# Splitting weights into high and low parts two k-tiles at a time in a two-layer recurrent decoder trunk

## The chip, the cores and the metric

The kernel runs on one core of a Trainium2 chip. The core has a matrix engine (TensorE, PE in the profile, with its weight loads as PEld), a vector engine (VectorE, DVE), a scalar engine (ScalarE, ACT), GpSimd (POOL), SyncE (SP, which only issues transfers here), and 16 DMA engines that move data between device memory (HBM) and the on-chip memories SBUF and PSUM. Each engine runs its own instructions in the order in which they stand and meets the others through semaphores. The metric is the device time of one execution in microseconds, as the median of several runs; lower is better.

## The reference

The reference computes a trunk of two residual layers on 256 positions of width 2048, all in float32. Each layer has two mixers that share one input and one output projection (layer 0: RWKV-7 and gated DeltaNet; layer 1: Mamba-2 and RG-LRU), then a gated feed-forward block with a short causal convolution (width 5632), then a gate that adds a normalised per-layer embedding.

```python
for i in range(DEPTH):                       # DEPTH = 2, x is (1, 256, 2048)
    y = even_mixer(x, ...) if i % 2 == 0 else odd_mixer(x, ...)
    h = layer_norm(DN_ALPHA * x + y, ln1_g[i], ln1_b[i])
    h = layer_norm(DN_ALPHA * h + conv_ffn(h, ffn_up[i], ffn_conv_w[i], ffn_conv_b[i], ffn_down[i]), ln2_g[i], ln2_b[i])
    e = rms_norm(p[i] @ ple_proj[i], ple_norm_g[i])
    x = h + jax.nn.sigmoid(h @ ple_gate_w[i] + ple_gate_b[i]) * e
```

All weights together are about 500 MB and each is used once.

## The kernel before

**The weight stream.** Every large product multiplies float32 weights by float32 activations with matmuls on the type `float32r`, which keeps fewer bits. To keep the precision, each operand is split into a high part (a cast to `float32r`) and a low part (the value less its high part), and three products are added: high by high, high by low, low by high. The activations are split once. The weights are split as they stream in: `wlist` lists all loads in order, 968 of them. One load (a granule, `granule`) brings two k-tiles, each 128 rows by 512 columns (416 or 464 in two of the projections), into a tile `wr` of 512 KB; four `wr` buffers exist (`PF`). ACT casts a k-tile into a tile `wh` (`self.scalar.copy`), DVE subtracts it from the raw weights into `wl`. Before the change each of these handles one k-tile.

**How far ahead.** `weights(name, p, k)` is called just before the matmuls of k-tile j are written out; it calls `ahead(j)`, which writes the casts up to k-tile j+5 and the subtractions up to k-tile j+4. Six `wh` and five `wl` buffers exist, so the cast of j+5 needs the buffer of j-1 back from PE.

**The products.** `down` makes a product with the activations as the stationary operand, six matmuls of 512 columns for each k-tile (bank `pd`). `up2` makes one with the weights stationary: four matmuls of 512 columns on `wh`, then four of 256 on `wl` (bank `pu`). `whole` adds the two halves of a bank of `up2`, over a small buffer `ph`.

**The order of the rest.** Everything else (post-processing of a bank, the mixers' own recurrences with their small matmuls, the layer norms) is written as tasks. A list scheduler (`pick`, `fill`, `need`) runs when the program is built: with a table of estimated costs it puts the tasks' instructions between the weight stream's, so that a small matmul stands where its inputs should be ready. The result is one fixed order for each engine. The casts and subtractions of `ahead` are not tasks: they stand where `ahead` is called.

**The layer norms.** At the end of the output projection and of the feed-forward block (four places) the last panel's sums (`x<-x,pd`) and their statistics (`st`, `mv`) go through DVE, the inverse root (`rstd`) and a product (`nmr`) through POOL, then rows are normalised on DVE (`x<-x,mv,rstd`) and ACT (`x<-x,nmr,rstd`), transposed on PE (bank `xt`) and scaled and split into `h` by ACT and DVE (`lv`). The next projection's matmuls wait for `h`. `down` with `early` writes the last four k-tiles of the panel for one half of the positions first, and two small panels (`pp`) give PE something to do meanwhile.

The functions that the diff touches:

Of the kernel before, what the change touches and what calls it, by code (L numbers as in the profile page):

```python
# [8 lines left out]
F32 = mybir.dt.float32  # L9
F32R = mybir.dt.float32r  # L10
AF = mybir.ActivationFunctionType
ALU = mybir.AluOpType
# [15 lines left out]
WSHAPES = {  # L28
# [5 lines left out]
    "lora": (1, 8, 464), "inA": (12, 4, 512), "inB": (16, 4, 512), "out0": (4, 8, 512),  # L34
    "zdt": (5, 8, 416), "xbc": (12, 4, 512), "inD": (16, 4, 512), "out1": (4, 16, 512),
}
# [32 lines left out]
class Pack:  # L69


    def __init__(self):
        self.at, self.cols, self.n = {}, [], 0
# [392 lines left out]
class Trunk(Scheduler):  # L466
    def __init__(self, ctx, tc, h, at, out, wlist):
        super().__init__(tc.nc)
        self.nc, self.h, self.at, self.out = self, h, at, out
        nc = self  # L470
        self.wlist = wlist
        self.wq = {key: i for i, key in enumerate(wlist)}
        self.n_dma = self.n_hi = self.n_lo = 0
        self.wt, self.wraw, self.names = {}, {}, {}
        self.loads = deque()
        pool = lambda name, bufs, **kw: ctx.enter_context(tc.tile_pool(name=name, bufs=bufs, **kw))
        self.cst = pool("cst", 1)
        self.wpool = pool("wp", 1)
        self.big = pool("big", self.NBIG)
        self.tmp = pool("tmp", 1)  # L480
        self.pm = pool("pm", 4, space=PSUM)
        self.pqp = pool("pq", self.NPQ, space=PSUM)
        self.dram = pool("dr", 1, space=DRAM)
        self.x1 = self.dram.tile([S, D], F32, name="x1")
        self.panel = 0
        self.done, self.used = {}, {}
        self.ident = self.cst.tile([128, 128], F32, name="ident")
        self.pk = self.cst.tile([128, h["pk"].shape[1]], F32, name="pk")
        self.cc = self.cst.tile([128, h["cst"].shape[1]], F32, name="cc")
        self.mhalf = self.cst.tile([128, 1], F32, name="mhalf")  # L490
        nc.gpsimd.memset(self.mhalf, -0.5)
        self.ones = self.cst.tile([128, 128], F32, name="ones")
        nc.gpsimd.memset(self.ones, 1.0)
# [52 lines left out]
        self.used[name] -= 1  # L546


    PF, SP, NBIG, LATE = 4, 4, 73, 4

    def granule(self, between=None):
        name, p, g = self.wlist[self.n_dma]
# [14 lines left out]
    def follow(self, t, tag, n):  # L567
# [4 lines left out]
            self.written[t.tensor.name] = [((t.tensor.name, 0, 128, 0, 1 << 20), end, None)]  # L572
        names.append(t.tensor.name)

    def ahead(self, j):

        n = 2 * len(self.wlist)
        while self.n_hi < min(n, j + self.SP + 2):
            i = self.n_hi // 2
            while self.n_dma < min(len(self.wlist), i + self.PF):  # L580
                self.granule()
            r = self.wraw[i][:, self.n_hi % 2, :WSHAPES[self.wlist[i][0]][2]]
            hi = self.wpool.tile([128, 512], F32R, tag="wh", bufs=self.SP + 2, name="wh")[:, :r.shape[1]]
            self.follow(hi, "wh", self.SP + 2)
            self.scalar.copy(hi, r)
            self.wt[self.n_hi] = [hi, r]
            self.n_hi += 1
        while self.n_lo < min(n, j + self.SP + 1):
            hi, r = self.wt[self.n_lo]
            lo = self.wpool.tile([128, 512], F32R, tag="wl", bufs=self.SP + 1, name="wl")[:, :r.shape[1]]  # L590
            self.follow(lo, "wl", self.SP + 1)
            self.vector.tensor_tensor(lo, r, hi.bitcast(F32), op=ALU.subtract)
            self.wt[self.n_lo][1] = lo
            self.n_lo += 1

    def weights(self, name, p, k):
        j = 2 * self.wq[name, p, k // 2] + k % 2
        self.ahead(j)
        self.wraw.pop(j // 2 - 1, None)
        return self.wt.pop(j)  # L600

    def post(self, gen, prio=0.0):
# [81 lines left out]
    def whole(self, ps):  # L684

        if ps.shape[1] == 512:
            t = self.tmp.tile([128, 256], F32, tag="ph", bufs=4, name="ph")
            self.scalar.copy(t, ps[:, 256:512])
            self.vector.tensor_tensor(ps[:, 0:256], ps[:, 0:256], t, op=ALU.add)
        return ps[:, 0:256]  # L690
# [1286 lines left out]
```

## Time and profile before

| | before |
|---|---|
| median of 3 runs | 2926.04 us (2923.46 to 2926.42) |
| the profiled execution's own time | 2927.23 us |
| its span (first to last instruction) | 2925.5 us |
| PE busy | 2898.3 us, 99% |
| DVE busy | 2158.3 us, 74% |
| ACT busy | 1735.9 us, 59% |
| DVE subtractions `wl<-wr,wh` | 1936, together 1318.5 us |
| ACT casts `wh<-wr` | 1936, together 1180.1 us |
| PE waits for the end of another engine or transfer | 11 pairs, longest in total 6.9 us |

A busy share is the union of an engine's instructions over the span. A matmul's record is longer than the distance to the next one, since they overlap, so the pace of PE is read from the starts.

### The profile page before, as it was taken

The page shows a single profiled execution, that of the slowest core. Times are in us where ns is not written, and L with a number is a line of the kernel's source. Part 1 is how long each engine was busy: PE and PEld are TensorE (multiplying, and loading weights), DVE is VectorE, ACT ScalarE, POOL GpSimd, SP SyncE. Part 2 cuts the span into 40 slices and gives each one's busy share as a digit, 9 for nine tenths or more (in the row PEclk, how much of TensorE's full clock was granted, in tenths as well). Part 3 has the DMA queues.
Part 4 walks back from the last instruction along what each step waited for, and adds up shares of the span by engine and source line. Part 5 has one row for each costly group of instructions (what it writes and reads, how often), then busy time and mean ns, then how long its engine had stood idle before and what let it go on. Part 6 is the DMA issues. An engine that isn't in the chain of part 4 may idle for free.

```text
span 2925.5 us, 48428 instructions
## 1 busy us (share of the span) xinstructions
PE 2898.3 (99%) x16986; PEld 2484.3 (85%) x16986; DVE 2158.3 (74%) x4246; ACT 1735.9 (59%) x3320; POOL 192.2 (7%) x317
## 2 busy tenths in 40 slices
PE   9999999999999999999999999999999999999999
PEld 8887887888888888888898888888888888888887
DVE  7789898687777775557856899855787777765567
ACT  6644555466666665446556778844666666654464
POOL 0133212000000000000000011000000000000000
PEclk9999999999999999999999999999999999999999
DMA  8554456465555556655776555666655555565556
GB/s 275 187 147 124 145 174 199 136 208 187 185 190 187 188 187 223 194 192 183 222 230 194 190 183 160 213 193 193 205 187 190 187 188 187 187 223 190 197 183 194
DMA packets 164949, 556.31 MB, mean 190 GB/s; under 512 B 19416, under 2 KB 32520, under 8 KB 164704
## 3 DMA queue, kind: packets, MB, share of 16 engines
q1 hardware_dynamic: 152128, 514.67, 53.9%
q0 software_dynamic: 12576, 38.55, 4.8%
q8 instruction: 133, 2.18, 0.3%
q14 instruction: 112, 0.92, 0.1%
HBM read 542.80 MB, written 10.34 MB: 189 GB/s over the span
## 4 chain that ended last, share of the span: by engine, by line
PE 93%; issue 2%; DMA 2%; DVE 2%; POOL 1%; ACT 0%; SPq 0%; POOLq 0%; DVEq 0%; ACTq 0%
PE pu L363 53%; PE pd L363 35%; DMA T<-inv 1%; PE s L363 1%; PE iv L363 1%; PE Y L363 1%; PE at L363 1%; PE lg L363 0%; PE tT L363 0%; PE xt L363 0%; POOL rstd L363 0%; DMA inv<-ix 0%; DMA inv<-AB 0%; PE R L363 0%; DVE wl L363 0%
## 5 line engine op out<-in xcount | busy, mean ns | idle before, releaser
L363 DVE TENSOR_TENSOR wl<-wr,wh 128x512 fp32r<-128x512 f32 (+2 forms) x1936 | 1318.5, 683 | 631.4 <-PE pd L363 312.5
L363 ACT CAST wh<-wr 128x512 fp32r<-128x512 f32 (+2 forms) x1936 | 1180.1, 618 | 892.9 <-PE pd L363 455.3
L363 PE MATMUL pu<-h,wh 128*128 128x512 f32 (+1 forms) x2944 | 781.5, 385 | 0.2
L363 PEld LDWEIGHTS pu<-h,wh 128*128 128x128 f32 x2944 | 499.2, 189 | 62.3 <-DVE h L363 0.6
L363 PEld LDWEIGHTS pu<-h,wl 128*128 128x128 f32 x2816 | 437.0, 189 | 57.3
L363 PE MATMUL pu<-h,wl 128*128 128x256 f32 x2816 | 463.8, 281 | 0.0
L363 PE MATMUL pu<-x,wh 128*128 128x512 f32 (+2 forms) x1024 | 281.8, 388 | 6.7 <-ACT wh L363 5.2
L363 PE MATMUL pd<-wh,acth 128*128 128x512 f32 x704 | 273.9, 389 | 0.0
L363 PE MATMUL pd<-wl,acth 128*128 128x512 f32 x704 | 273.9, 389 | 0.0
L363 PE MATMUL pd<-wh,actl 128*128 128x512 f32 x704 | 273.9, 389 | 0.0
L363 PE MATMUL pu<-xT,wh 128*128 128x512 f32 x896 | 250.3, 398 | 1.0 <-ACT xb L363 0.6
L363 PE MATMUL pd<-wh,yT 128*128 128x512 f32 x768 | 241.2, 391 | 0.0
L363 PEld LDWEIGHTS pu<-x,wh 128*128 128x128 f32 (+1 forms) x1024 | 172.7, 189 | 29.1 <-ACT wh L363 5.2
L363 PE MATMUL pu<-x,wl 128*128 128x256 f32 (+1 forms) x960 | 172.4, 288 | 0.0
L363 PEld LDWEIGHTS pu<-xT,wh 128*128 128x128 f32 x896 | 153.2, 189 | 22.0 <-ACT xb L363 0.9
L363 PEld LDWEIGHTS pd<-wh,yT 128*128 128x128 f32 x768 | 144.2, 188 | 30.5 <-issue 1.0
L363 PEld LDWEIGHTS pu<-x,wl 128*128 128x128 f32 (+1 forms) x960 | 150.5, 189 | 20.6 <-issue 1.5
L363 PE MATMUL pd<-wh,h 128*128 128x512 f32 x512 | 162.4, 393 | 0.0
L363 PEld LDWEIGHTS pd<-wh,acth 128*128 128x128 f32 x704 | 132.1, 188 | 27.6
L363 PEld LDWEIGHTS pd<-wl,acth 128*128 128x128 f32 x704 | 132.1, 188 | 27.4
L363 PEld LDWEIGHTS pd<-wh,actl 128*128 128x128 f32 x704 | 132.1, 188 | 27.3
L363 PEld LDWEIGHTS pu<-xT,wl 128*128 128x128 f32 x896 | 137.7, 189 | 19.5 <-issue 0.7
(409 smaller groups left out, 3214.3 us busy)
## 6 DMA issues: line engine op xcount, KB each, us to landing
wr<-in_up SPq DMA_DIRECT2D x336, 512.0 KB, 3.3
wr<-in_dn SPq DMA_DIRECT2D x176, 512.0 KB, 3.6
wr<-in_out SPq DMA_DIRECT2D x96, 512.0 KB, 4.2
wr<-in_inB SPq DMA_DIRECT2D x64, 512.0 KB, 3.5
wr<-in_gw SPq DMA_DIRECT2D x64, 512.0 KB, 3.9
wr<-in_inD SPq DMA_DIRECT2D x64, 512.0 KB, 4.2
wr<-in_inA SPq DMA_DIRECT2D x48, 512.0 KB, 4.1
wr<-in_xbc SPq DMA_DIRECT2D x48, 512.0 KB, 4.0
```

Of the source, the lines that this page charges most:

```text
L363: getattr(x.eng, op.name)(*op.a, **op.k)
```

## The change

One cast and one subtraction now handle a whole granule, that is both k-tiles (128 x 2 x 512). `wh` and `wl` become tiles of two k-tiles with three buffers each (`HI`). At the even k-tile of granule g, `ahead` writes the cast of granule g+2; at the odd one the subtraction of granule g+2. Only the very first granule is still split in two steps (`apart`). In SBUF, `wh` takes the same room, `wl` 2 KB more for each partition, and the buffers of `ph` go from 4 to 2 to pay for it.

```diff
-    PF, SP, NBIG, LATE = 4, 4, 73, 4
+    PF, HI, NBIG, LATE = 4, 3, 73, 4
...
+    @staticmethod
+    def apart(i):
+
+        return [slice(0, 2)] if i else [slice(0, 1), slice(1, 2)]
+
     def ahead(self, j):
 
-        n = 2 * len(self.wlist)
-        while self.n_hi < min(n, j + self.SP + 2):
-            i = self.n_hi // 2
-            while self.n_dma < min(len(self.wlist), i + self.PF):
+        n, g = len(self.wlist), j // 2
+        while self.n_hi < min(n, g + self.HI):
+            i = self.n_hi
+            while self.n_dma < min(n, i + self.PF):
                 self.granule()
-            r = self.wraw[i][:, self.n_hi % 2, :WSHAPES[self.wlist[i][0]][2]]
-            hi = self.wpool.tile([128, 512], F32R, tag="wh", bufs=self.SP + 2, name="wh")[:, :r.shape[1]]
-            self.follow(hi, "wh", self.SP + 2)
-            self.scalar.copy(hi, r)
-            self.wt[self.n_hi] = [hi, r]
+            w = WSHAPES[self.wlist[i][0]][2]
+            hi = self.wpool.tile([128, 2, 512], F32R, tag="wh", bufs=self.HI, name="wh")
+            self.follow(hi, "wh", self.HI)
+            for a in self.apart(i):
+                self.scalar.copy(hi[:, a, :w], self.wraw[i][:, a, :w])
+            self.whi[i] = hi
             self.n_hi += 1
-        while self.n_lo < min(n, j + self.SP + 1):
-            hi, r = self.wt[self.n_lo]
-            lo = self.wpool.tile([128, 512], F32R, tag="wl", bufs=self.SP + 1, name="wl")[:, :r.shape[1]]
-            self.follow(lo, "wl", self.SP + 1)
-            self.vector.tensor_tensor(lo, r, hi.bitcast(F32), op=ALU.subtract)
-            self.wt[self.n_lo][1] = lo
+        while self.n_lo < min(n, g + self.HI - 1 + j % 2):
+            i = self.n_lo
+            w = WSHAPES[self.wlist[i][0]][2]
+            raw, hi = self.wraw.pop(i), self.whi.pop(i)
+            lo = self.wpool.tile([128, 2, 512], F32R, tag="wl", bufs=self.HI, name="wl")
+            self.follow(lo, "wl", self.HI)
+            for a in self.apart(i):
+                self.vector.tensor_tensor(lo[:, a, :w], raw[:, a, :w], hi.bitcast(F32)[:, a, :w], op=ALU.subtract)
+            for a in range(2):
+                self.wt[2 * i + a] = hi[:, a, :w], lo[:, a, :w]
             self.n_lo += 1
...
-            t = self.tmp.tile([128, 256], F32, tag="ph", bufs=4, name="ph")
+            t = self.tmp.tile([128, 256], F32, tag="ph", bufs=2, name="ph")
```

Since the scheduler goes by costs, the whole order of the tasks moves with it. The first place that matters below is DVE at the end of layer 0's feed-forward block, from the last panel's first sum to the first normalised rows. Before:

```order
L363 SCALAR_TENSOR_TENSOR x<-x,pd 128x512
L363 TENSOR_TENSOR wl<-wr,wh 128x512
L363 BN_STATS st<-x 128x6
L363 TENSOR_TENSOR wl<-wr,wh 128x512 x2
L363 SCALAR_TENSOR_TENSOR x<-x,pd 128x512
L363 TENSOR_TENSOR wl<-wr,wh 128x512
L363 BN_STATS st<-x 128x6
L363 TENSOR_TENSOR wl<-wr,wh 128x512
L363 BN_AGGR mv<-st 128x2 x2
L363 TENSOR_TENSOR wl<-wr,wh 128x512
L363 TENSOR_SCALAR x<-x,mv,rstd 128x512 x2
L363 TENSOR_TENSOR wl<-wr,wh 128x512
```

DVE at the same place with the change:

```order
L363 SCALAR_TENSOR_TENSOR x<-x,pd 128x512
L363 TENSOR_TENSOR wl<-wr,wh 128x1024
L363 BN_STATS st<-x 128x6
L363 TENSOR_TENSOR wl<-wr,wh 128x1024
L363 SCALAR_TENSOR_TENSOR x<-x,pd 128x512
L363 BN_STATS st<-x 128x6
L363 TENSOR_TENSOR wl<-wr,wh 128x1024
L363 BN_AGGR mv<-st 128x2 x2
L363 TENSOR_SCALAR x<-x,mv,rstd 128x512
L363 TENSOR_TENSOR wl<-wr,wh 128x1024
L363 TENSOR_SCALAR x<-x,mv,rstd 128x512 x2
L363 TENSOR_SCALAR lv<-xt,pk 128x256
```

A subtraction of a whole granule now stands between the normalised rows of the first and of the second half of the positions, where before both stood together. The same order is found at the other three layer norms.

The second place is ACT there, from the small panel's copy (`e`, `sq`) to the first parts of `h`. Before:

```order
L363 COPY e<-pd 128x512
L363 ACTIVATE sq,ss_5624<-pd 128x512
L363 ACTIVATE x<-x,nmr,rstd 128x512
L363 CAST wh<-wr 128x512
L363 ACTIVATE h<-xt,pk 128x256 x3
```

ACT there with the change:

```order
L363 COPY e<-pd 128x512
L363 ACTIVATE sq,ss_4991<-pd 128x512
L363 COPY e<-pd 128x512
L363 ACTIVATE x<-x,nmr,rstd 128x512 x2
L363 ACTIVATE sq,ss_4992<-pd 128x512
L363 ACTIVATE h<-xt,pk 128x256 x2
```

A second normalised row block and a second `sq` now stand ahead of the first `h`, and a cast of one k-tile has left.

## Rows read from the trace of the kernel before

**Rows 1.** Page, busy time: us, share of the span, instructions.

```profile
PE 2898.3 (99%) x16986; PEld 2484.3 (85%) x16986; DVE 2158.3 (74%) x4246; ACT 1735.9 (59%) x3320; POOL 192.2 (7%) x317
```

**Rows 2.** PE's waits, whole span: who <- for whom: us in total, times, longest.

```profile
PE iv L363 <- DMA T<-inv: 6.9, 6, 1.9
...
PE xt L363 <- DVE lv L363: 2.4, 4, 0.7
PE pu L363 <- ACT x L363: 1.3, 1, 1.3
PE tT L363 <- DVE ix L363: 1.1, 1, 1.1
```

**Rows 3.** Chain that ended last: start, us, what; layer 0's second feed-forward product.

```profile
1113.76 242.12 PE pd L363 x1068
```

**Rows 4.** Timeline of PE inside that stretch: start, us, instruction.

```profile
1199.99 0.39 PE L363 MATMUL pd<-wh,acth 128*128 128x512 f32 x1
1200.21 0.39 PE L363 MATMUL pd<-wl,acth 128*128 128x512 f32 x1
1200.44 0.39 PE L363 MATMUL pd<-wh,actl 128*128 128x512 f32 x1
```

**Rows 5.** Groups by shape: instruction, count, busy us, mean ns, idle before.

```profile
L363 DVE TENSOR_TENSOR wl<-wr,wh 128x512 fp32r<-128x512 f32 x1840 | 1262.0, 687 | 592.7 <-PE pd L363 291.2 <-PE pu L363 216.8 <-issue 56.4
L363 ACT CAST wh<-wr 128x512 fp32r<-128x512 f32 x1840 | 1128.8, 622 | 850.2 <-PE pd L363 422.3 <-PE pu L363 364.0 <-ACT wh L363 34.3
...
L363 DVE TENSOR_TENSOR wl<-wr,wh 128x416 fp32r<-128x416 f32 x80 | 46.4, 590 | 33.5 <-PE pd L363 21.4 <-ACT wh L363 11.5 <-issue 0.3
...
L363 ACT CAST wh<-wr 128x416 fp32r<-128x416 f32 x80 | 42.1, 540 | 36.9 <-PE pd L363 33.0 <-DMA wr<-in_zdt 2.9 <-DVE spw L363 0.6
```

**Rows 6.** Timeline of DVE at layer 0's second layer norm.

```profile
1353.47 0.68 DVE L363 SCALAR_TENSOR_TENSOR x<-x,pd 128x512 f32<-128x512 f32 x1
1354.07 0.68 DVE L363 TENSOR_TENSOR wl<-wr,wh 128x512 fp32r<-128x512 f32 x1
...
1355.87 0.38 DVE L363 BATCH_NORM_AGGREGATE mv<-st 128x2 f32<-128x24 f32 x2
...
1357.62 1.17 DVE L363 TENSOR_SCALAR x<-x,mv,rstd 128x512 f32<-128x512 f32 x2 [0.83 <-POOL rstd L363]
```

**Rows 7.** Timelines of ACT and PE at the same place.

```profile
1358.88 0.81 ACT L363 ACTIVATE x<-x,nmr,rstd 128x512 f32<-128x512 f32 x1 [1.27 <-POOL nmr L363]
1360.11 1.47 ACT L363 ACTIVATE h<-xt,pk 128x256 fp32r<-128x256 f32 x3
1361.93 0.62 ACT L363 ACTIVATE sq<-pd 128x512 f32<-128x512 f32 x1
...
1358.43 2.13 PE L363 MATMUL xt<-ident,x 128*128 128x128 f32 x12
1361.60 0.47 PE L363 MATMUL pd<-wh,h 128*128 128x512 f32 x1
```

**Rows 8.** Timelines of ACT, DVE and PE in layer 1's first panels.

```profile
1506.24 0.98 ACT L363 CAST wh<-wr 128x416 fp32r<-128x416 f32 x2 [4.92 <-PE pd L363]
...
1506.82 1.09 DVE L363 TENSOR_TENSOR wl<-wr,wh 128x416 fp32r<-128x416 f32 x2 [4.45 <-ACT wh L363]
...
1507.55 0.37 PE L363 MATMUL pd<-wl,xT 128*128 128x416 f32 x1
```

**Rows 9.** Timeline of PE where four small matmuls have just stood in the stream.

```profile
1488.97 0.44 PE L363 MATMUL pd<-wh,xT 128*128 128x416 f32 x1
1489.24 0.35 PE L363 MATMUL pd<-wl,xT 128*128 128x416 f32 x1
1489.43 0.35 PE L363 MATMUL pd<-wh,xT 128*128 128x416 f32 x1
```

**Rows 10.** Windows: length; busy PE, PEld, DVE, ACT, POOL (instructions); granted clock; DMA.

```profile
1700.00:1846.00 146.00, 145.18 (x935) 123.71 (x933) 134.56 (x282) 118.17 (x237) 13.89 (x19) 1.00 0.52 164
206.48:209.89 3.41, 3.41 (x31) 2.90 (x31) 1.43 (x4) 0.37 (x1) 1.77 (x1) 0.50 0.02 5
```

More of the change, by code (lines that the diff above doesn't have):

```diff
@@ L473, in __init__ @@
         self.n_dma = self.n_hi = self.n_lo = 0
-        self.wt, self.wraw, self.names = {}, {}, {}
+        self.wt, self.wraw, self.whi, self.names = {}, {}, {}, {}
         self.loads = deque()
@@ L598, in weights @@
         self.ahead(j)
-        self.wraw.pop(j // 2 - 1, None)
         return self.wt.pop(j)
```

## The prediction

> **What bounds the kernel now.** I read the page's busy times first, then who waits for whom on PE, then the chain that ended last, and only then single stretches.
>
> PE is busy for 2898.3 of 2925.5 us [rows 1], so all of its idle time is 27 us. The list of PE's waits says what that idle time is [rows 2]. The longest pair (6.9 us, six times) is a small matmul of a mixer waiting for a transfer that brings back an inverted block. Another 2.4 us, four times, is the transposes of the four layer norms. There is no row in which PE waits for a weight in mid-stream.
>
> A busy PE need not run at its best pace, so I looked at a stretch without any side work: 1,068 matmuls of 512 columns in 242.12 us, 226.7 ns each [rows 3]. At 2.4 GHz 512 columns take 213.3 ns, so 13 ns for each matmul are not array time. The question is whether the change can touch them. The starts say no [rows 4]: of the six matmuls of a k-tile, the one that first reads a new `wh`, the one that first reads a new `wl`, and one whose operands are long there follow each other at 0.22 to 0.23 us alike. If operands were late, the first reader would show it.
>
> By the Trainium skill, "TensorE: Matmul & The Clock Gate", section "Wait — 56ns, not 53.3ns?", a warm matmul of 512 columns starts 215.7 ns after the one before it; the 1,068 matmuls would then take 230.4 us. That rule would leave 11.7 us in this stretch for something else to give back. The trace does not agree on the pace, and the equal starts decide against weights as the cause.
>
> DVE (74%) and ACT (59%) are off the bound. Their idle time before `wl` and `wh` is mostly a wait for PE to give a buffer back [rows 5]: they run ahead as far as buffers allow.
>
> **The change part by part.** *Fewer, longer instructions.* A k-tile's subtraction takes 687 ns for 512 columns and 590 for 416 [rows 5], so 1.01 ns a column, and 1024 columns cost about 687 + 517 = 1204 ns in place of 1374: 0.17 us less for each of 968 granules, 165 us of DVE. For ACT, 622 and 540 ns give 0.854 ns a column, 1059 ns in place of 1244, 179 us of ACT. On the path this is worth nothing: the matmul stream hides it, and cover is lost only where a side chain waits for DVE or ACT.
>
> *How far ahead.* A k-tile is six matmuls, 1.36 us [rows 3]. Before, the subtraction of k-tile j+4 can start when k-tile j starts and is needed 4 x 1.36 + 0.23 us later; less 0.69 us that leaves 5.0 us. With the change the granule's buffer comes back at the same moment, but cast and subtraction of the whole granule follow each other, 1.06 + 1.20 us, so 3.4 us are left. I take no cost in the stream; the first rival is that this fails.
>
> *The four layer norms.* Here DVE's chain is on the path, and the order shows subtractions in it. I follow layer 0's second norm, all from its own times [rows 6, 7]. DVE starts back-to-back instructions 0.60 us apart for 512 columns, so about 1.13 for 1024. The last sum before the statistics starts at 1353.47 now. With the change it stands behind a granule's subtraction whose cast has to wait for PE to leave the granule two before; that ends about 1354.1, so +0.6. The aggregate moves from 1355.87 to about 1356.4 (+0.5), the first normalised rows from 1357.62 to 1358.15. The second half's rows start 0.6 us after the first now, and 1.7 us after with a whole subtraction in between: +1.6 us in all. ACT gets its product 0.5 us later, so its first rows move from 1358.88 to 1359.4; then a second row block (0.72 apart) and a `sq` with its read-out (0.7) come before the first `h`, which moves from 1360.11 to about 1361.55. The first matmul on `h` so moves from 1361.60 to about 1362.2, and its low part, which has DVE behind ACT, by about 0.95 us. By then PE has done four transposes fewer (0.35 us). I take +1.3 us for each norm. The bounds: 0, if PE's transposes can all be done in the wait, and 2.0, if the 1.6 us and the four transposes pass through whole. Four norms: +5.2 (0 to 8).
>
> *The first panel.* The low part of the third k-tile's activation now stands on DVE behind a subtraction of two tiles of 464 columns instead of one, about 0.5 us more by the same slope [rows 5], and PE already waits there (1.3 us [rows 2]): +0.5.
>
> *A late transfer.* In layer 1's first panels one granule lands so late that its cast starts at 1506.24, its subtraction at 1506.82, and PE reads the result at 1507.55, at once [rows 8]. Cast and subtraction of 832 columns by the slopes take 0.90 + 1.01 us where the first half took 0.54 + 0.59, so +0.7 (0 to 1.5).
>
> *Fewer interruptions.* Counted in PE's order, small matmuls cut into the stream 194 times before and 172 times with the change; the matmuls are the same. After one such cut the next matmul starts 0.27 us later where 0.19 is the pace [rows 9], so 0.08 us each, -1.8 us for 22.
>
> *Side chains.* Waits for inverted blocks and for `ix` are 8.0 us [rows 2]. In layer 1's busiest stretch DVE works 134.56 of 146 us [rows 10]; about 52 granules pass there, so it loses 9 us and falls from 92% to 86%. A less loaded DVE comes closer to the costs that the order was made with. I take -1.0; bounds -8 (all gone) and +8 (as much again). Clock dips belong here: in 206.48 to 209.89 the granted clock is 0.50, 1.2 GHz, after PE had waited for an inverted block, which costs half of 3.41 us [rows 10]. I count on as many as now.
>
> The smaller `ph` costs nothing in my sum: the two copies of a panel meet two buffers, and the sums that free them are made a panel earlier (8 k-tiles, over 10 us).
>
> **The sum.** 5.2 + 0.5 + 0.7 - 1.8 - 1.0 = +3.6 us. On the profiled execution's own time, 2927.23 us, that is 2930.8; this execution was 1.2 us above the median of 2926.04, so on the median I forecast 2929.6 us, 0.12% more. About 0.2% (5.9 us) is what a measurement of this kernel can tell from no change.
>
> **The rivals.** *1. The stream starves.* The margin of 3.4 us fails where DVE or ACT are late by more than that at a granule. It decides in the mixers, where DVE is at 92% [rows 10] and a subtraction queues behind several side instructions. If each of the 52 granules there came 0.2 us too late, PE would lose 10.4 us: 2940. Against it: today's 5.0 us leave no wait at all there, and DVE gets less to do.
>
> *2. The relief reaches PE.* The side chains wait less, the 8.0 us fall to 2 and both clock dips go (3.4 us), and the norms cost only half of my term: -6.0 - 3.4 + 2.6 + 0.5 + 0.7 - 1.8 = -7.4, 2918.6. For it: the waits of the mixers are for chains of many short DVE instructions. Against it: six of the waits are for transfers, which don't get faster, and a longer subtraction also delays each short instruction behind it.
>
> *3. Nothing moves.* The norms' delay is hidden, and the other terms cancel (0.5 + 0.7 - 1.8 - 1.0): -1.6, 2924.4.
>
> *4. Operands set the pace after all.* If the 13 ns for each matmul were waiting, and half of it went with half of the semaphores, the 1,068 matmuls would gain 7 us and the 16,986 instructions of PE some 90: about 2835. The equal starts speak against it [rows 4].
>
> **How the numbers follow.** The forecast's mechanism (an unchanged stream, norms somewhat longer) gets 0.56, with its own range 2925 to 2936; nothing moves 0.14; starvation 0.16; relief 0.12; the pace 0.02. Slower by over 0.2% (above 2931.9) takes nearly all of starvation and a third of the forecast: 0.34. Faster (below 2920.2) takes two thirds of relief and the pace: 0.10. The rest, 0.56, is within 0.2%. The range of 8 in 10 goes from 2919, into relief, to 2939, nearly the starvation case.
>
> **What would show it.** Right: about 970 subtractions near 1.20 us and as many casts near 1.06 us; DVE near 2,000 us busy, ACT near 1,560; the stretch of 1,068 matmuls again 242.1 us; at the norms the first `pd` on `h` about 1 us later after the end of the small panels, with PE's wait for `x` or ACT's `h` grown from 2.4 us to 6 or more. Wrong: PE waiting for `wl` or `wh` in the mixers; a different pace in the unbroken stretch; more or fewer dips of the granted clock; norms as short as now.

## The result, and the profile after

| | before | after |
|---|---|---|
| median (range) | 2925.9 us (2923.46 to 2926.42), 4 runs | 2946.24 us (2941.41 to 2950.48), 4 runs |
| ratio to before, 95% interval | | 1.0071 (1.0059 to 1.0083) |
| profiled execution, its span | 2927.23 us, 2925.5 us | 2950.48 us, 2948.7 us |
| mean granted clock of that span | 0.998 | 0.993 |

The change makes the kernel 0.7% slower. The forecast was 2929.6 us, with a range up to 2939.

The page's busy times after (us, share of the span, instructions; before in [rows 1]), and the by-form groups of the casts and subtractions (busy us, mean ns of one | idle us of the engine ahead of them, and who ended it; before in [rows 5]):

```profile
PE 2908.5 (99%) x16986; PEld 2493.9 (85%) x16986; DVE 2049.2 (69%) x3279; ACT 1599.8 (54%) x2360; POOL 196.2 (7%) x317
```

```profile
L363 ACT CAST wh<-wr 128x1024 fp32r<-128x1024 f32 x920 | 967.8, 1052 | 955.7 <-PE pd L363 485.6 <-PE pu L363 416.4 <-issue 22.5
...
L363 DVE TENSOR_TENSOR wl<-wr,wh 128x1024 fp32r<-128x1024 f32 x920 | 1122.6, 1221 | 512.3 <-ACT wh L363 510.2 <-DVE grow L363 0.2
```

DVE lost 109 us of busy time, ACT 136 (158 and 176 by forecast). What is new stands behind the bar: DVE's idle time ahead of a subtraction now ends with the subtraction's own cast, no longer with a buffer that PE gives back.

PE's waits after (who <- for whom: us in total, times, longest; before in [rows 2]):

```profile
PE iv L363 <- DMA T<-inv: 11.5, 4, 8.3
...
PE xt L363 <- DVE x L363: 4.1, 4, 1.0
PE pd L363 <- ACT h L363: 2.3, 2, 1.2
PE pu L363 <- ACT h L363: 2.3, 2, 1.2
...
PE pu L363 <- DVE h L363: 1.3, 2, 0.7
...
PE pd L363 <- DVE wl L363: 0.6, 2, 0.4
...
PE pd L363 <- DVE h L363: 0.6, 2, 0.3
```

The waits on `xt` and `h` belong to the four norms. Waits for `wl` come to 0.6 us.

**Where the 23 us went.** The matrix products come in the same order in both kernels. So I compare the start of the n-th stream matmul (`pu` or `pd`) in the two traces; the difference is how far the changed kernel lags at that point of the work:

| stretch of the work | lag at its start and end, us | half clock after, us | half clock before, us |
|---|---|---|---|
| layer 0 up to the small panels of the first norm | 0 to 12.9 | 10.24 + 17.07 | 3.41 + 3.41 |
| first norm | 12.9 to 16.5 | 3.41 | 0 |
| feed-forward of layer 0 | 16.5 to 16.5 | 0 | 0 |
| second norm | 16.5 to 19.2 | 3.41 | 0 |
| layer 1's mixer | 19.2 to 18.4 | 0 | 0 |
| third norm | 18.4 to 21.6 | 3.41 | 0 |
| feed-forward of layer 1 | 21.6 to 21.6 | 0 | 0 |
| fourth norm to the end | 21.6 to 23.0 | 2.66, at the very end | 1.98, at the very end |

The half-clock columns are read from the windows view, where the granted clock stands under PEclk (from:to, length, then busy us and instructions of PE, PEld, DVE, ACT, POOL, PEclk, DMA share, GB/s):

```profile
338.25:348.49 10.24, 9.55 (x95) 7.42 (x97) 3.90 (x9) 4.21 (x6) 0.00 (x0) 0.50 0.42 108
498.68:515.75 17.07, 13.66 (x170) 10.09 (x172) 6.65 (x12) 2.08 (x4) 4.36 (x6) 0.50 0.43 109
631.80:635.21 3.41, 3.41 (x17) 3.41 (x18) 3.41 (x9) 2.93 (x8) 0.51 (x1) 0.50 0.89 233
640.00:1360.00 720.00, 720.00 (x3860) 621.49 (x3859) 459.77 (x648) 380.39 (x536) 4.27 (x8) 1.00 0.59 192
1379.32:1382.73 3.41, 3.12 (x11) 2.38 (x11) 3.41 (x9) 2.84 (x6) 0.00 (x0) 0.50 0.01 5
2106.36:2109.77 3.41, 3.41 (x18) 3.41 (x17) 3.41 (x8) 2.46 (x6) 0.00 (x0) 0.50 1.02 309
2110.00:2840.00 730.00, 730.00 (x3917) 630.28 (x3916) 464.02 (x653) 386.46 (x543) 4.27 (x8) 1.00 0.59 193
```

PEclk is 0.50, that is 1.2 GHz, in five stretches that begin in or behind waits of PE, and 1.00 through both feed-forward streams, where the lag does not move by 0.1 us in 720 us. A stretch at half clock costs half its length if PE would have worked all through. The four norms lag 10.9 us: 5.1 us of that are half of three times 3.41 us, and 5.8 are waiting. In the longest stretch PE works 13.66 of 17.07 us: it stands through the first 3.41 us, the end of a wait, which is lost at either clock. Counting only the time in which PE works, the five stretches cost 16.6 us, 13.2 more than the two before.

The same can be done for every run without its trace: time less span times (1 - mean granted clock). I call it the time at full clock; the clock is listed to 0.001, so one value is good to 1.5 us. The four runs of the changed kernel (clock 0.993 to 0.996) give 2928.2 to 2929.8, mean 2929.2. The 65 runs of the kernel before beside the experiments below (0.996 or more) give 2920.3 in the mean. So of some 20 us about 9 are waiting and 11 are clock. The clock's part is an upper bound, since this sum charges half of a stretch also where PE stands in it.

**The norm.** DVE and PE at layer 0's second norm, after (timeline: start, us, instruction [idle before <- who ended it]; before in [rows 6, 7]):

```profile
1374.29 0.55 DVE L363 TENSOR_SCALAR x<-x,mv,rstd 128x512 f32<-128x512 f32 x1 [0.94 <-POOL rstd L363]
1374.75 1.22 DVE L363 TENSOR_TENSOR wl<-wr,wh 128x1024 fp32r<-128x1024 f32 x1
1375.88 1.00 DVE L363 TENSOR_SCALAR x<-x,mv,rstd 128x512 f32<-128x512 f32 x2
```

```profile
1376.48 1.09 PE L363 MATMUL xt<-ident,x 128*128 128x128 f32 x8 [1.04 <-DVE x L363]
1378.73 0.50 PE L363 MATMUL pd<-wh,h 128*128 128x512 f32 x1 [1.16 <-ACT h L363]
```

The subtraction stands between the rows, as its order showed; PE waits for the rows behind it, then for ACT's `h`.

**The output projection of layer 0.** PE, and POOL's queue there:

```profile
492.79 0.98 PE L363 MATMUL iv<-T,AB 64*64 64x64 f32 x28
502.09 0.28 PE L363 MATMUL iv<-iP,T 32*32 32x32 f32 x2 [8.32 <-DMA T<-inv]
```

```profile
485.17 4.37 POOL L363 DMA_DIRECT2D x<-in_x  x8
490.31 0.72 POOL L363 DMA_DIRECT2D T<-inv  x1 [0.77 <-DMA x<-in_x]
491.21 0.70 POOL L363 DMA_DIRECT2D T<-inv  x1 [0.17 <-issue]
```

PE waits 8.32 us for an inverted block `T`. Its loads stand behind the eight loads of the residual rows `x`, 256 KB each. The load issued at 490.31 us lands at 501.95, 11.64 us later and just behind the last `x` (501.24); the loads of `T` in the same stretch with no `x` just ahead of them take 2.9 to 3.3 us. In the order of the kernel before, four of the last eight loads of `T` stood ahead of the `x` loads; here two.

### The profile page after: what moved, and what is told of

The parts are those of the page before. It is cut to its first block, busy times and chain, and to the rows that moved or that the text cites. A ratio compares the mean times of both kernels' runs of the same rounds, so it can differ in the third digit from the quotient of the medians.

```text
span 2948.7 us, 44553 instructions
## 1 busy us (share of the span) xinstructions
PE 2908.5 (99%) x16986; PEld 2493.9 (85%) x16986; DVE 2049.2 (69%) x3279; ACT 1599.8 (54%) x2360; POOL 196.2 (7%) x317
## 4 chain that ended last, share of the span: by engine, by line
PE 93%; DVE 2%; issue 2%; DMA 2%; POOL 1%; ACT 1%; SPq 0%; DVEq 0%; POOLq 0%; ACTq 0%
PE pu L363 54%; PE pd L363 33%; PE iv L363 1%; DMA T<-inv 1%; PE s L363 1%; DVE wl L363 1%; POOL rstd L363 1%; PE Y L363 1%; PE at L363 1%; PE xt L363 0%; PE lg L363 0%; PE tT L363 0%; PE lo L363 0%; DMA wr<-in_zdt 0%; PE O L363 0%
## 5 line engine op out<-in xcount | busy, mean ns | idle before, releaser
L363 DVE TENSOR_TENSOR wl<-wr,wh 128x1024 fp32r<-128x1024 f32 (+2 forms) x969 | 1172.7, 1211 | 553.9 <-ACT wh L363 551.5
L363 ACT CAST wh<-wr 128x1024 fp32r<-128x1024 f32 (+2 forms) x969 | 1011.3, 1044 | 1006.2 <-PE pd L363 519.8
L363 DVE TENSOR_TENSOR pu<-pu,ph 128x256 f32<-128x256 f32 x280 | 107.0, 426 | 175.0 <-ACT ph L363 174.7
L363 PEld LDWEIGHTS pu<-xT,wh 128*128 128x128 f32 x896 | 153.0, 189 | 21.3 <-ACT xb L363 0.9
```

The costliest lines, as they stand in the source:

```text
L363: getattr(x.eng, op.name)(*op.a, **op.k)
```

## The experiments

My first theory, A: the loss is order. The 1.22 us subtraction at the norms, and the `x` loads ahead of `T`, make PE wait, and the clock falls behind the waits. Rivals: B, the new place at which a pair of splits is issued, whatever its width; C, width alone. All runs beside each other. The ratio is to runs of the kernel before taken beside each run. Waits and half clock are from the profiled execution; waits are PE's idle time in us, with the pauses that are too short for a bracket in the timeline; "norms" runs from 5 us before the first transpose of each of the four to 35 us behind it, "projection" from 470 us to the first norm:

| run | median us | ratio (95%) | at full clock | norms | projection | half clock, us |
|---|---|---|---|---|---|---|
| before | 2925.9 | 1 | 2920.3 | 3.6 | 1.9 | 8.8 |
| after | 2946.2 | 1.0071 (1.0059-1.0083) | 2929.2 | 10.6 | 9.2 | 40.2 |
| e1_norm_halves | 2947.0 | 1.0064 (1.0048-1.0080) | 2930.1 | 9.7 | 8.3 | 15.5 |
| e2_all_halves | 2940.5 | 1.0051 (1.0039-1.0063) | 2931.7 | 9.7 | 6.8 | 16.3 |
| e3_x_by_panel | 2941.7 | 1.0063 (1.0048-1.0079) | 2927.6 | 10.4 | 4.1 | 23.6 |
| e3b_before_x_by_panel | 2927.2 | 1.0003 (0.9994-1.0011) | 2922.1 | 3.6 | 1.4 | 14.3 |
| f5_norm_lo_early | 2953.0 | 1.0115 (1.0096-1.0133) | 2939.8 | 15.2 | 7.5 | 17.7 |
| f4b_wide_cast_only | 3019.9 | 1.0320 (1.0306-1.0334) | 2978.8 | 13.1 | 32.7 | 63.8 |
| h_before_lat180 | 2944.3 | 1.0064 (1.0051-1.0077) | 2929.1 | 6.0 | 11.4 | 23.2 |
| h_after_lat180 | 2943.0 | 1.0061 (1.0048-1.0074) | 2930.6 | 10.5 | 1.0 | 27.2 |
| f2_lo_even | 2946.0 | 1.0061 (1.0048-1.0075) | 2931.4 | 16.6 | 6.2 | 30.6 |
| f2b_lo_even_x_by_panel | 2946.8 | 1.0068 (1.0055-1.0080) | 2932.6 | 16.0 | 3.5 | 31.5 |
| h_after_lat200 | 2937.6 | 1.0034 (1.0022-1.0047) | 2926.4 | 10.9 | 1.2 | 21.3 |
| k_before_added_waits | 2947.3 | 1.0071 (1.0058-1.0083) | 2934.0 | 3.6 | 0.2 | 23.8 |
| f8_single_subs_later | 2938.1 | 1.0038 (1.0024-1.0052) | 2927.2 | 5.2 | 2.7 | 23.3 |
| h_before_lat180_x_by_panel | 2948.1 | 1.0081 (1.0068-1.0095) | 2932.4 | 6.0 | 13.0 | 34.0 |
| h_before_lat200 | 2927.8 | 1.0008 (0.9999-1.0017) | 2920.3 | 3.6 | 0.9 | 7.9 |
| p_before_ph2 | 2925.5 | 1.0004 (0.9995-1.0013) | 2919.9 | 3.6 | 1.4 | 4.4 |
| f8_lat200 | 2945.5 | 1.0066 (1.0053-1.0079) | 2932.5 | 5.4 | 7.0 | 38.0 |
| f8_lat180 | 2946.8 | 1.0076 (1.0063-1.0090) | 2928.6 | 6.6 | 14.4 | 36.5 |

**Width: halves at the norms (e1), halves everywhere (e2).**

```diff
-        return [slice(0, 2)] if i else [slice(0, 1), slice(1, 2)]
+        near = i == 0 or any(b - 4 <= i < b + 10 for b in (152, 418, 668, 934))
+        return [slice(0, 1), slice(1, 2)] if near else [slice(0, 2)]
```

e2 returns the two halves always.

> The changed kernel, with casts and subtractions in halves for the 14 loads around each of the four norms, wide elsewhere. Theory A (at a norm the 1.22 us subtraction stands on VectorE between two row operations and keeps TensorE waiting): the norms cost +3.6, +2.7, +3.3 and +1.4 us more than in the kernel before, 10.9 in all, and come back to within 1 us of it each: 2946.2 - 7 to - 10 = 2936 to 2939 us, with no TensorE wait over 0.8 us and no half clock at the last three norms. Rival B (placement: buffers of whole loads and the new point at which a split is issued, whatever the width): norms stay, 2945 to 2948 us. Layer 0's mixer should stay as it is in both, 12.9 us behind the kernel before.

> The changed kernel with every cast and subtraction in halves: buffers and call sites of the change, widths of the kernel before. In its program the eight loads of x still stand on POOL's queue ahead of loads of T (four of T directly behind them). Theory A (the loss in layer 0's mixer is POOL's order, not width; the loss at the norms is width): mixer still behind by 8 to 17 us, norms within 1 us each: 2934 to 2943 us. Rival C (width alone: side chains lengthened by 1.2 us operations): mixer and norms both as before, 2924 to 2930 us. Rival B (placement alone, norms too): 2943 to 2949 us.

Theory A failed at the norms. DVE and PE at the second norm of e2:

```profile
1364.95 1.23 DVE L363 TENSOR_TENSOR wl<-wr,wh 128x512 fp32r<-128x512 f32 x2
1366.81 2.08 DVE L363 TENSOR_SCALAR x<-x,mv,rstd 128x512 f32<-128x512 f32 x4 [0.64 <-POOL rstd L363]
1370.43 0.55 DVE L363 TENSOR_SCALAR lv<-xt,pk 128x256 f32<-128x256 f32 x1 [1.54 <-ACT h L363]
```

```profile
1367.41 2.06 PE L363 MATMUL xt<-ident,x 128*128 128x128 f32 x12 [0.76 <-DVE x L363]
1371.03 0.33 PE L363 MATMUL xt<-ident,x 128*128 128x128 f32 x1 [1.55 <-DVE lv L363]
```

Two halves in one go (1.23 us) take as long as one whole (1.22 us), the norms wait 9.7 us as against 10.6, and the time at full clock is no better. Width is not the cause; C falls. B stands by the waits, though e2's 2940.5 us, with less half clock, lies below B's range and inside A's.

**The loads of x.** e3 issues them two at each panel of the projection's first part; e3b does so in the kernel before.

```diff
-        for q in range(4):
-            for t in range(2):
-                self.gpsimd.dma_start(out=s[t][q], in_=src[t * 128:t * 128 + 128, q * 512:q * 512 + 512])
...
+                if n == 0:
+                    self.rows_in(src, s, p)
```

> The changed kernel with the loads of the residual rows x issued two at each panel of the first part of the output projection, not all eight ahead of its first panel; all else in the order of layer 0's mixer stays, so that two loads of x and not eight stand ahead of the last six loads of T. Theory A: TensorE's wait of 8.3 us at 494 us and the 17 us at half clock behind it go, 8 + 8.5 us less, a few us given back where the panel's own x is late: 2928 to 2934 us. Rival C (T is late because the wide operations hold up the chain that feeds it): the wait stays above 5 us, 2942 to 2947 us.

> The kernel before with the same edit of the loads of x. There the last four loads of T stood behind the x loads too, and TensorE didn't wait for them. Theory A: 2924 to 2928 us, no change. Rival D (the loads of x always cost several us by their share of the memory): faster by 3 to 8 us, 2918 to 2923 us.

The wait for `T` went, as A said, but 3.46 us for DVE's `ys` took its place at 492 us, and the norms' half clock stayed. The time fell by 4.5 us, 1.6 us at full clock, where A promised 12 or more; the intervals of the two ratios overlap, so even this fall is not clear of noise. In the kernel before the loads cost nothing.

**Where the pair stands at a norm.** f5 issues the subtraction one k-tile earlier around the norms, together with its cast; f2 issues it one k-tile later everywhere; f2b is f2 with e3's edit.

```diff
-        while self.n_lo < min(n, g + self.HI - 1 + j % 2):
+        while self.n_lo < min(n, g + self.HI - (0 if near else 1 - j % 2)):
...
-        while self.n_lo < min(n, g + self.HI - 1 + j % 2):
+        while self.n_lo < min(n, g + self.HI - 1):
```

> The changed kernel, whole widths, but around the four norms the subtraction of a load is issued one k-tile earlier, together with its cast, so that on VectorE's queue it stands ahead of the row operations, not between the first and the second. Theory P (what costs at the norms is the place in the queue at which two k-tiles' split is put, not its width): the TensorE waits at a norm, 2.5 to 2.9 us in the changed kernel, fall to 1.5 us or less each; by time less the clock's shortfall (time minus span times one minus the mean granted clock; 2929 in the changed kernel, 2920.5 before) 2923 to 2926, by time 2936 to 2942 us, since layer 0's mixer keeps its half clock. Rival W (a 1.2 us operation anywhere near the norm keeps TensorE waiting): waits 2.3 to 2.9 us still, 2942 to 2950 us.

> The changed kernel with each load's subtraction issued one k-tile later: two k-tiles behind its cast instead of one. In the changed kernel VectorE stands idle 551 us ahead of subtractions for the cast of the same load (0 us in the kernel before, where it waited there for TensorE's buffers). Theory Q (these waits in VectorE's queue hold up the side chains that stand behind them): the idle time for casts falls below 150 us, layer 0's mixer has fewer TensorE waits than the changed kernel (13 us between 150 and 600 us), and time less the clock's shortfall falls from 2929 to 2922 to 2926; by time 2928 to 2938 us. In this order the x loads still stand ahead of seven loads of T on POOL's queue, so a wait for T of some us may stay. Rival M (the lead of the low parts over TensorE, 3.4 us in the changed kernel, falls by a k-tile of 1.36 us and is too short): TensorE waits for wl of 3 us or more in all, 2945 to 2960 us. Rival N (no matter where the subtraction stands): 2941 to 2950 us.

> The kernel with the subtraction one k-tile later, and the loads of x two at each panel. Theories A and Q together: no TensorE wait for T over 3 us near 490 us, VectorE's idle time for casts below 150 us, 2926 to 2936 us. Rival M: as in the run without the edit of x.

Both made the norms worse, 15.2 and 16.6 us. In f5 the rows stood together behind the pair, and PE waited 1.47 us for them and again further on; its 2953.0 us lies above the ranges of P and W alike. In f2 one wait, for `lv`, was 3.88 us:

```profile
1370.05 1.05 PE L363 MATMUL xt<-ident,x 128*128 128x128 f32 x4 [3.88 <-DVE lv L363]
```

Moving the pair moves the wait. f2 also refutes Q: a k-tile more of distance left DVE's idle time for casts at 501 us. It waits for the cast where it had waited for a buffer, as the casts themselves wait for PE's buffers (the group of casts above).

**Pairs or singles.** f4b has casts of a whole load and a subtraction for each k-tile, issued where the kernel before did, at the same k-tile as the cast. f8 has the same casts, and each single subtraction one k-tile later.

```diff
-        while self.n_lo < min(n, g + self.HI - 1 + j % 2):
+        while self.n_lo < min(2 * n, j + 4):
```

(f4b has `j + 5`; in both, `i, a = divmod(self.n_lo, 2)` picks the half. f4b also keeps `wl` in five buffers of one k-tile, f8 in three of two.)

> The part of the change that ScalarE sees: casts of a whole load, but a subtraction for each k-tile, issued where the kernel before issued it (ph has two buffers as in the change, 74 units instead of 73 with the room left). Theory P for the subtractions (what the pairs on VectorE's queue cost): TensorE waits at the norms back to 1.5 us or less each, and time less the clock's shortfall within 2 us of 2920.5 plus what the other order of the mixer makes, by time 2924 to 2932 us. Rival (it is the paired casts on ScalarE): waits at the norms 2.3 us or more, 2934 to 2946 us.

> Casts of a whole load as in the change, but subtractions for each k-tile, one at every k-tile, one k-tile later than in the kernel before (so that each stands one or two k-tiles behind its cast). On VectorE's queue the norms then have the order of the kernel before (one subtraction, two row operations, one subtraction, one row operation), and on POOL four of the last eight loads of T stand ahead of the loads of x. Theory P (two subtractions in one go, wide or not, are what costs at the norms): waits at each norm 1.5 us or less, VectorE's idle time for casts under 150 us, 2922 to 2931 us. Rival (the paired casts on ScalarE cost at the norms): waits of 2 us or more at each, 2934 to 2945 us. Rival M (lead too short): TensorE waits for wl of 3 us or more in all.

f4b was the worst of all. DVE now stands 755 us for casts, as against 510 in the changed kernel:

```profile
L363 DVE TENSOR_TENSOR wl<-wr,wh 128x512 fp32r<-128x512 f32 (+2 forms) x1936 | 1295.0, 684 | 780.1 <-ACT wh L363 755.1 <-PE pu L363 6.7 <-PE pd L363 0.6
```

It says nothing against the casts, because f8 keeps them and has norms of 5.2 us, 1.6 above the kernel before. Which of the two differences between f4b and f8, the place or the buffers, makes f4b so slow is not shown. DVE and PE in f8:

```profile
1367.09 1.16 DVE L363 TENSOR_SCALAR x<-x,mv,rstd 128x512 f32<-128x512 f32 x2 [0.83 <-POOL rstd L363]
1368.17 0.68 DVE L363 TENSOR_TENSOR wl<-wr,wh 128x512 fp32r<-128x512 f32 x1
1368.77 0.54 DVE L363 TENSOR_SCALAR x<-x,mv,rstd 128x512 f32<-128x512 f32 x1
```

```profile
1368.31 1.71 PE L363 MATMUL xt<-ident,x 128*128 128x128 f32 x11 [0.23 <-DVE x L363]
1370.93 0.55 PE L363 MATMUL xt<-ident,x 128*128 128x128 f32 x3 [0.92 <-DVE lv L363]
```

Of the 7.0 us of waits that the change adds at the norms, 5.5 go with the pairing of subtractions, and no half clock follows the norms in f8 or in its two other orders below (5.4 and 6.6 us). The place of a pair matters less: in the table every kernel with pairs waits 9.7 to 16.6 us at the norms, wherever they stand, and every kernel with singles, f4b aside, 3.6 to 6.6. My expectation of f8's time (to 2931) failed, for its mixer waits and has 20.5 us at half clock. So did that of DVE's idle time for casts (under 150 us): it is 521 us, and the norms are short all the same.

**Other orders of the mixer.** One constant of the scheduler's model, the latency between engines, is set to 180 or 200 ns; the operations stay. h_before_lat180_x_by_panel adds e3's edit.

```diff
-LAT = 190.0
+LAT = 180.0
```

> The kernel before with one number of the scheduler's model changed, its latency between engines from 190 to 180 ns: the same operations, in a somewhat other order. In this order the eight loads of x stand on POOL's queue ahead of the last eight loads of T, as they stood ahead of six in the changed kernel. Theory A (order on POOL): a TensorE wait for T of 5 us or more near 490 us, and 5 to 15 us slower, 2931 to 2941 us. Rival L (the order of the mixer hardly matters as long as the width and pairing are those of before): within 2 us, 2924 to 2928 us.

> The changed kernel with that same number at 180 ns. In this order four of the last eight loads of T stand ahead of the loads of x on POOL's queue, as in the kernel before; the norms keep the order of the changed kernel. Theory A: no wait for T over 2 us near 490 us, norms as in the changed kernel (2.5 to 2.9 us of waits each): 2933 to 2940 us. Rival (pairing slows the whole mixer, whatever the queue's order): 2941 to 2950 us.

> The changed kernel with the scheduler's latency at 200 ns instead of 190. On POOL four of the last eight loads of T stand ahead of the loads of x; at the norms one subtraction now stands ahead of all five row operations instead of between the first and the second. Theory A and the place at the norm: mixer without a wait for T over 2 us near 490 us; norms with a wait ahead of the first transposes of 0.7 to 1.5 us and 2 to 2.9 us in all, as in the kernel with halves. 2935 to 2945 us. If the place between the first two row operations is what costs: norms 1.5 us or less each, 2930 to 2937 us.

> The kernel before at 200 ns. In this order four of the last eight loads of T stand ahead of the loads of x, as in the kernel before. Theory A (what makes orders of the mixer differ by over 10 us is these loads): no wait for T over 2.5 us near 490 us, 2921 to 2930 us. Rival (any other order than that of the kernel before costs 10 us or more): 2935 us or more.

> The kernel before at 180 ns of the scheduler's latency, which took 2944.3 us with a wait for T of 8.86 us at 493 us, with the loads of x two at each panel. Theory A: the wait falls to 3 us or less, 2928 to 2936 us. Rival (the T loads are late for another reason): wait over 6 us, 2940 to 2946 us.

> Paired casts and single subtractions as before, the scheduler's latency at 200 ns. The norms should again cost the kernel before's time plus 2 to 3 us in all (0.4 to 0.9 us each). In this order the loads of x stand on POOL's queue ahead of all of the last eight loads of T. Theory A (such an order costs at the output projection): TensorE waits of 5 us or more between 480 and 580 us, 2934 to 2945 us. Rival (their place decides nothing, the mixer's time differs from order to order for other reasons): any time between 2924 and 2945 us, without a wait for T over 2.5 us there.

> The same at 180 ns; the loads of x stand ahead of all of the last eight loads of T here too. Theory A: waits of 5 us or more between 480 and 580 us, 2934 to 2945 us. Rival: as in the other run.

The kernel before is 19 us slower in another order (2925.0 beside it), with no change to any operation. Three orders of it take 2920.3, 2929.1 and 2920.3 us at full clock (latency 190, 180, 200), three of the changed kernel 2929.2, 2930.6 and 2926.4. So the changed kernel is the slower one on the whole, but its 9 us at full clock are no more than the spread of the old one. PE there, and with the `x` loads spread:

```profile
502.19 0.44 PE L363 MATMUL iv<-T,AB 64*64 64x64 f32 x2 [8.86 <-DMA T<-inv]
```

```profile
574.64 1.09 PE L363 MATMUL tT<-ident,oc 128*128 128x128 f32 x4 [5.17 <-DVE oc L363]
579.22 1.12 PE L363 MATMUL tT<-ident,oc 128*128 128x128 f32 x4 [3.48 <-DVE oc L363]
```

In the eight kernels with all eight `x` loads ahead of six or more of the last eight `T` loads (after, e1, e2, f5, h_before_lat180, f2, f8_lat200, f8_lat180) PE waits 6.2 to 14.4 us at the projection (f4b, of this group too, 32.7); in the seven with four `T` loads ahead of them (before, h_before_lat200, p_before_ph2, k_before_added_waits, h_after_lat180, h_after_lat200, f8) 0.2 to 2.7. So the place of these loads goes with the waits there. It does not settle the time: h_after_lat180 waits 1.0 us there and takes 2930.6 us at full clock, the changed kernel 9.2 us and 2929.2, and the rival's range (2941 to 2950 us) held its 2943.0, not A's. Nor is the wait always for `T`: the longest one is for `oc` in e2, for `ys` in f2 and for `sw` in f8_lat180. In the kernel before in the slower order, spreading the loads moved the wait 76 us on, to `oc`, without a gain. I read them as a mark, which no run shows: the projection is begun while more of the side chains is still to do, and one of their links is then waited for. What puts the chains behind in one order and not in another stays open.

**Waits and the clock.** Copies of a bank hold the start of four panels in the down projections, in mid-stream.

```diff
+        for _ in range({("dn0", 1): 1, ("dn0", 2): 3, ("dn1", 1): 6, ("dn1", 2): 13}.get((name, p), 0)):
+            self.vector.tensor_copy(ps[0], self.prev[1])
```

> The kernel before, with 1, 3, 6 and 13 copies of a bank on VectorE that TensorE has to wait for at the starts of the second and third panels of the two down projections, in the middle of streams with no other wait (their values are overwritten). By 0.68 us for one such operation the waits should be about 1, 2.4, 4.4 and 9.2 us, 17 us in all. Theory K (a wait of TensorE is followed by a stretch at half clock, whatever the work around it, longer behind longer waits): stretches at 0.5 begin at or behind at least the three longer waits, 3.4 to 17 us each, and the time is 17 us plus 4 to 16 us over the kernel before: 2946 to 2960 us. Rival (half clock comes with the small matmuls and transposes of the side chains, not with waits): no stretch below full clock in the down projections, 2942 to 2945 us.

PE's four added waits are 0.89, 2.35, 4.55 and 9.69 us (17.5 in all). Two of them, and the windows view around three:

```profile
2645.13 0.77 PE L363 MATMUL pd<-wh,acth 128*128 128x512 f32 x1 [4.55 <-DVE pd L363]
...
2717.30 0.76 PE L363 MATMUL pd<-wh,acth 128*128 128x512 f32 x1 [9.69 <-DVE pd L363]
```

```profile
1222.00:1240.00 18.00, 15.65 (x69) 12.68 (x68) 11.85 (x19) 7.01 (x12) 0.00 (x0) 1.00 0.49 172
2643.34:2650.16 6.82, 5.03 (x12) 4.00 (x13) 5.25 (x9) 0.62 (x1) 0.00 (x0) 0.50 0.13 43
2711.60:2721.84 10.24, 4.54 (x11) 3.60 (x12) 9.00 (x14) 0.62 (x1) 0.00 (x0) 0.50 0.04 9
```

The half clock begins within each of the two long waits and lasts beyond it; at the two short ones there is none (one less than K said). A wait alone can bring the clock down, with nothing but matmuls of 512 columns around it. At half clock the 12 matmuls of the first stretch take 5.03 us, 0.42 us each as against 0.227. By the Trainium skill, "TensorE: Matmul & The Clock Gate", section "HAM oscillation — how this bites in real kernels", a stream that waits for its data goes on at half the clock and loses half of such a stretch. These rows agree. They also show what the time at full clock hides: this run has 13.7 us more of it than the kernel before, where the waits add 17.5, because PE stands in 7.5 of the 17.06 us at half clock and half of that was taken off as well.

**The smaller ph alone**, two buffers in the kernel before:

> The kernel before with two buffers of ph instead of four, the last part of the change by itself; every engine's queue keeps its order. If two buffers are enough: 2924 to 2928 us. If the copies wait for a free ph: 2930 us or more, with VectorE or ScalarE idle ahead of ph.

No change. No version here beats the kernel before; the best with whole-load operations is h_after_lat200, 2937.6 us.

## Why the prediction was wrong

**The step that failed** is "I count on as many [clock dips] as now", within the side-chain term of -1.0. In place of two stretches of 3.41 us the changed kernel had five, 37.5 us together; by the time at full clock they cost 11 us more in the mean of the runs, by the profile 13 to 15. The next is the term itself: it took a less loaded DVE to bring shorter waits in the mixers, while the new order decides that, and this one waits 9.2 us at the projection where the old one waits 1.9. Most of that was made up elsewhere in the mixers, as the last but one item shows. Why this order comes to the projection late stays open.

Step by step:
- *Sizes.* Right: 1211 ns a subtraction over all forms, 1044 ns a cast; ACT is 40 us busier than said, DVE 49. The subtractions alone lost 146 us; a busy share is a union, and on DVE fewer instructions now overlap at their ends.
- *The stream.* Right: no lag in either feed-forward block, waits for `wl` 0.6 us in all. The margin of 3.4 us was enough. The rival of starvation fell, and so did that of the operands' pace: the chain's unbroken stretch in the same product shows 226.7 ns a matmul again. Relief did not come.

```profile
1130.23 236.68 PE pd L363 x1044
```

- *The norms.* Right in size at full clock (+5.2 forecast, +5.8 measured) and in mechanism down to the subtraction between the rows; but I priced the wait and not the 5.1 us of half clock behind three of them. Where I wrote 1.2 us for a longer instruction it should have been "two subtractions at one place": e2 has it with short ones.
- *First panel and late transfer.* Right: lag 0.7 to 0.8 us after the first panel (+0.5 said), 0.4 + 0.25 us for the late granule (+0.7 said).
- *Fewer interruptions and side chains* (-2.8 together). Without the clock the rest of the kernel came to about +0.5: the profile's lag of 23.0 us, less half of the 30.7 us that it has more at half clock, is 7.6; less 5.8, 0.7 and 0.65 that leaves 0.5. With the clock charged only where PE works it is 9.8, and 2.5 are left. Either way the -2.8 did not come.
- *ph.* Right, shown by itself.

So the sum at full clock was +3.6 by forecast, 7.6 to 9.8 in the profile and 8.9 in the mean of the runs; with as many dips as before, 2926 + 8.9 would have been inside the range. The range ended at 2939 because none of my cases joined a bad order with the clock behind it.

## What to carry to other kernels

Where a scheduler lays out the rest of the kernel, changing one operation's size can change every order, and the order can be worth as much as the edit, as it was here: run the old kernel in two or three disturbed orders first to learn that spread. Price a wait of the matrix engine with the half clock that can follow it, and split a comparison of two runs into waiting and clock before looking for causes, without charging the clock for time in which the engine stands. Here work taken off an engine that was not the bound was worth nothing by its sum; what counted was how much of it stood at one place ahead of a short chain, and batching two pieces put twice as much there.

## What was not expected of the hardware

The length of a half-clock stretch is not fixed by the wait: behind nearly equal waits (8.32 us and 7.46 us) for the same transfer, the changed kernel had 17.07 us at half clock and e1, with the same order there, 6.8 us. Four runs of one program differed by 9 us in time and by 1.7 us at full clock. At the second norm, waits of 1.04 and 1.16 us with transposes between them were followed by 3.41 us at half clock, while the same two waits at the fourth norm were not, and neither was one wait of 2.35 us in mid-stream. Why the same waits bring the clock down at one place and not at another is not shown.
